# First half's feed-forward operand normalised behind its merge; second half's y, x and old operand on GpSimd's DMA queue

## The chip, the cores and the metric

The kernel runs on one core of a Trainium2 chip. The metric is the device time of one execution in microseconds (us). PE is TensorE (matrix products), DVE is VectorE, ACT is ScalarE, POOL is GpSimd, SP is SyncE, which here only issues DMAs. ACT and POOL issue DMAs too.

## The reference

One decoder layer over 1024 tokens of width 1024, in fp32: two mixers side by side, merged by gates, then a SwiGLU feed-forward block, then a norm.

```python
u = rmsnorm(h, norm1_g); proj = u @ w_in
y_a = rwkv7_mix(token_shift(p_rwkv, tshift_mu), ...)      # a recurrence over tokens
y_b = dsa_attention(q, k, v, q_idx, k_idx, w_idx)          # causal, top-256 keys
g_a, g_b = jnp.split(jax.nn.sigmoid(p_gate), 2, axis=-1)
h = h + (g_a * (y_a @ w_o_rwkv) + g_b * (y_b @ w_o_att)) @ w_out
z = rmsnorm(h, norm2_g) @ w_ffn_in                         # 1024 x 5632
z_gate, z_up = jnp.split(z, 2, axis=-1)
h = h + (jax.nn.silu(z_gate) * z_up) @ w_ffn_out           # 2816 x 1024
return rmsnorm(h, normf_g)
```

rmsnorm divides each token's row by its root mean square and multiplies it by a gain for each column.

## The kernel before

**Tiles and products.** The tokens are worked in two halves of 512. Activations lie transposed: a tile is 128 channels by 512 tokens, and eight of them are one half of a 1024-wide operand. To keep fp32 precision each product runs in three passes on a high and a low part of both operands: `split` writes `hi` on ACT (L117) and `lo = x - hi` on DVE (L118), and `mm3` issues hi x hi (L143), hi x lo (L144) and lo x hi (L148), 24 matmuls for eight blocks of 128, 18 for six. Weights stream in through `wst` (three buffers) and are split the same way into `whi` and `wlo` (two buffers each). Products go to PSUM: `acc()` takes one of three banks in turn, `mix()` one of five. `tmp()` is a ring of four tiles.

**Order.** PE's order is written by hand: the program issues the matmuls of the long chains (rwkv, attention) itself and between them pumps work from a queue named `fill`. On the other engines and the DMA queues a scheduler sets the order beforehand; each works its list in order, and waits where the next entry isn't ready.

**The stages around the change.** While rwkv and attention of the second half run, `fill` holds `merge` and `ffn` of the first half. `merge(0)` forms h, stores it as `d_h`, and writes z = h times the gain of norm2 as the parts zhi and zlo, not yet divided by the root mean square. That divisor comes as a `row` (1 x 512, spread over the partitions; L276) only when `ffn_in` is under way, so each gate product pg and up product pu of `ffn_in` is multiplied by `row` as it leaves PSUM (L1289 to L1293). The feed-forward width is worked in three groups of 8, 8 and 6 blocks (`GROUPS`), each with `ffn_in` (j over the blocks, two products each) and `ffn_out` (d over eight output blocks, added to `d_h`; L1315 loads the old value, L1321 adds, L1325 stores). Beside the last `ffn_out` of the first half the helper `scaled` multiplies z by `row`, splits it anew and stores it as `d_z` (L1442 to L1445).

Then `merge(1)` runs for the second half (it loads y at L1201 and x in `load_x`), and `joint` works the third group of both halves together with fewer products, as in Strassen's method. It needs sums and differences of both halves' operands: `old(k)` loads a block of `d_z` (L1543), L1534 normalises the second half, L1560 and L1566 form the sums. The results go to `d_f`. `reload` brings them back, and the final `ffn_out` adds the last product of the first half, in three `acc` banks of which the second half's `ffn_in`, pumped ahead and suspended, holds two.

Of the kernel before, what the change touches and what calls it, by code (L numbers as in the profile page):

```python
# [24 lines left out]
HT = 512  # L25
# [25 lines left out]
def block_kernel(ctx: ExitStack, tc: tile.TileContext, ins: dict, outT: bass.AP, outR: bass.AP, stop=None, dbg=None):  # L51
# [55 lines left out]
    def acc():  # L107
        return psA.tile([128, HT], F32, tag="acc", name="acc")
# [4 lines left out]
    def tmp():  # L113
        return tp.tile([128, HT], F32, tag="tmp", name="tmp")
# [167 lines left out]
        A.activation(hi, x, AF.Copy, scale=g)  # L282
        V.scalar_tensor_tensor(lo, x, g, hi.bitcast(F32), op0=ALU.mult, op1=ALU.subtract)

    def load_x(half, h, js):
        src = ins["xT"][:, half * HT:(half + 1) * HT].rearrange("(k p) t -> p k t", p=128)
        for j in js:
            SY.dma_start(h[:, j, :], src[:, j, :])

# [906 lines left out]
    def merge(half, zp, zs, between=None):  # L1196
        yt = yhi, ylo = act_tiles(zp, "y", ("s0", "s1"))
        mt = act_tiles(zp, "m", ("s2", "s3"))
        for j in range(8):
            t = ylo[:, j, :].bitcast(F32)  # L1200
            SY.dma_start(t, (d_ya if j < 4 else d_yb)[half][j % 4])  # L1201
            split(yhi[:, j, :], ylo[:, j, :], t)
        yield (-30, -56)[half]
        for d in range(8):
            w = weights(ins["w_o"][d])
            ga, gb = tmp(), tmp()
            SY.dma_start(ga, d_g[half][d])
# [12 lines left out]
        h = zp.tile([128, 8, HT], F32, tag="s0", name="h")  # L1220
        load_x(half, h, range(8))
        sq = Rms(h)
        zt = zhi, zlo = act_tiles(zp, "z", ("s1", "s3")) if half == 0 else (None, None)
        pss = []
        if half == 0:
            pss = [acc(), acc()]
            yield from mm3_last(pss, [weights(ins["w_out"][d]) for d in range(2)], mt, 8)
        for d in range(8):
            if d == 4 and between:
                between()  # L1230
            if d < len(pss):
# [12 lines left out]
        for d in range(8):  # L1244
            V.scalar_tensor_tensor(zlo[:, d, :], h[:, d, :], par[:, P_N2 + d:P_N2 + d + 1],
                                   zhi[:, d, :].bitcast(F32), op0=ALU.mult, op1=ALU.subtract)
        zs.extend((zt, sq))
# [12 lines left out]
                T.matmul(ps, whi[:, k, :], alo[:, k, :], start=False, stop=k == 7)  # L1260
            yield 8

    def ffn_in(f, zs, gi):

        z, sq = zs[:2]
        g0, gn = GROUPS[gi]
        for j in range(gn):
            pg, pu = acc(), acc()
            src = [ins["w_ffn_in"][2 * (g0 + j) + i] for i in range(2)]
            if gi == j == 0 and sq is not None:  # L1270
                ws = [weights(x) for x in src]
                first_ = mm3_late([pg, pu], ws, z)
                for i, n in enumerate(first_):
                    yield n
                    if i == 3:
                        sq.columns()
                zs.append(sq.row())
                yield 4
            else:
                yield from mm3(pg, weights(src[0]), z)  # L1280
                yield from mm3(pu, weights(src[1]), z)
            t = tmp()
            if sq is None:
                A.activation(t, pg, AF.Tanh, scale=0.5)
                V.scalar_tensor_tensor(t, t, 1.0, pg, op0=ALU.add, op1=ALU.mult)
                V.scalar_tensor_tensor(t, pu, 0.5, t, op0=ALU.mult, op1=ALU.mult)
            else:
                row, x = zs[2], tmp()
                V.tensor_tensor(x, pg, row, op=ALU.mult)  # L1289
                A.activation(t, x, AF.Tanh, scale=0.5)  # L1290
                V.scalar_tensor_tensor(t, t, 1.0, x, op0=ALU.add, op1=ALU.mult)
                V.scalar_tensor_tensor(x, pu, 0.5, row, op0=ALU.mult, op1=ALU.mult)
                V.tensor_tensor(t, t, x, op=ALU.mult)  # L1293
            split(f[0][:, j, :], f[1][:, j, :], t)

    def ffn_out(half, zp, f, gi, sqs=None):
        gn = GROUPS[gi][1]
        final = sqs is not None
        if final:
            h = zp.tile([128, 8, HT], F32, tag="s1", name="h")  # L1300
            sqs.append(Rms(h))
            for d in range(8):
                G.dma_start(h[:, d, :], d_h[half][d])

        def w(d):
            return weights(ins["w_fo1"][d] if final else ins["w_fo0"][gi, d], gn)

        pss = [acc() for _ in range(1 if final else 2)]
        yield from mm3_last(pss, [w(d) for d in range(len(pss))], f, gn, within=half == 1)
        for d in range(8):  # L1310
            if final:
                t = h[:, d, :]
            else:
                t = tmp()
                SY.dma_start(t, d_h[half][d])  # L1315
            if d < len(pss):
                ps = pss[d]
            else:
                ps = acc()
                yield from mm3(ps, w(d), f, nk=gn)  # L1320
            V.tensor_tensor(t, t, ps, op=ALU.add)  # L1321
# [100 lines left out]
            V.tensor_scalar(out[:, 512:768], hT[:, 512:768], rs, None, op0=ALU.mult)  # L1422
            SY.dma_start(outR[:, 512:1024], out[:, 512:1024])

    def ffn(half, zp, zs, tags, after=None):

        for gi in range(JOINT):
            f = act_tiles(zp, "f", tags)
            yield from ffn_in(f, zs, gi)
            side = iter(after() if after and gi == JOINT - 1 else ())  # L1430
            for n in ffn_out(half, zp, f, gi):
                yield n
                next(side, None)
            for _ in side:
                pass

    def scaled(z, row):

        zhi, zlo = z
        for k in range(8):  # L1440
            hi, lo, t = zhi[:, k, :], zlo[:, k, :], tmp()
            V.tensor_tensor(t, hi.bitcast(F32), lo.bitcast(F32), op=ALU.add)  # L1442
            V.tensor_tensor(t, t, row, op=ALU.mult)
            split(hi, lo, t)
            SY.dma_start(d_z[k], t)  # L1445
            yield

    class Planes:


        def __init__(self, *aps):
            self.aps = aps

        def __getitem__(self, at):
            return self.aps[at[1]][:, at[2]]

    def parts(t):
        return [t[:, k, :] for k in range(4)], [t[:, 4 + k, :] for k in range(4)]

    def joint(z0, zp0, zs1, zp1, md, after):  # L1460

# [78 lines left out]

        def old(k):
            t = tmp()
            SY.dma_start(t, d_z[k])  # L1543
            return t

        def less(k):
# [24 lines left out]
        run(*fill)  # L1571
        fill.clear()
        credit[0] = 0
        b11, b21 = ([[x[:, k, :] for k in ks] for x in z0] for ks in (range(4), range(4, 8)))
        with tc.high_priority():
            first_rows(0)
            first_rows(1)
# [2 lines left out]
            m2(j)  # L1580

        def rest():
            t3, T3 = pair(zp0, "s2")
            for k in range(4):
                split(t3[:, k, :], t3[:, 4 + k, :], less(k))
            t4, T4 = pair(zp0, "s0")
# [53 lines left out]
    def reload(half, f):  # L1640
        for j in range(GROUPS[JOINT][1]):
            t = f[1][:, j, :].bitcast(F32)
            SY.dma_start(t, d_f[half][j])
            split(f[0][:, j, :], f[1][:, j, :], t)

    def chain(*gens):
# [61 lines left out]
    def ready():  # L1708
# [5 lines left out]
        zps.append(opened("left", "zp0"))  # L1714
        m = merge(0, zps[0][1], z0)
        next(m)
        fill.append(chain(m, ffn(0, zps[0][1], z0, ("s2", "s0"), lambda: scaled(z0[0], z0[2]))))

    rwkv(1, rp, consts, ready)
    wq[0] = SY  # L1720
# [111 lines left out]
```

## Time and profile before

| what | value |
|---|---|
| time, median of three runs | 1784.09 us (1781.21 to 1787.59) |
| profiled execution | 1781.26 us, span 1779.4, granted clock 0.985 |
| PE busy | 1699.8 us |
| DVE busy | 1149.3 us |
| ACT busy | 869.2 us |
| POOL busy | 104.3 us |
| waits of PE for L1321's tmp | 25.7 us in two waits |
| waits of PE for L1321's h | 13.1 us in seven waits |

The span is the time between the first and the last instruction of the profiled execution. A timeline row gives start, length, engine, line, operation, what it writes and reads, and in brackets how long the engine stood before it and which instruction ended that. Consecutive matmuls overlap: each row's length is longer than the distance to the next.

### The profile page before, as it was taken

To read this page: it belongs to the slowest core of one execution; us is meant where nothing else is said; L and a number is where in the kernel's file an instruction comes from. 1 tells how busy PE (TensorE), PEld (TensorE's weight loads), DVE (VectorE), ACT (ScalarE), POOL (GpSimd) and SP (SyncE) were. 2 spreads that over 40 slices of the span, in tenths; PEclk is the share of its full clock that TensorE was granted. 3 is DMA by queue.
4 is the path that set the end of the run, shared out by engine and by line. 5 is a ranking of instruction groups with operands and counts; after the bars stand their busy time and mean duration, and the time that the engine had idled before them with its cause. 6 is when DMAs were issued, how large, how long until landed. Compare 5 with 4: busy or idle time off the path is not lost.

```text
span 1779.4 us, 26713 instructions
## 1 busy us (share of the span) xinstructions
PE 1699.8 (96%) x10000; PEld 1395.9 (78%) x10000; DVE 1149.3 (65%) x2242; ACT 869.2 (49%) x1685; POOL 104.3 (6%) x127
## 2 busy tenths in 40 slices
PE   8999999999999999999999999699699997999998
PEld 7888888888877777787878888577578775888888
DVE  6789899865577578778856655665775543433334
ACT  5365997543555887654343655323233342222322
POOL 0000000010021110001002110000000000000001
PEclk9999999999999999999999999899899999999999
DMA  5542344454376336633437652556622442453363
GB/s 209 183 132 80 107 112 146 141 131 151 110 223 180 111 122 199 202 111 97 123 113 230 156 148 71 184 170 196 183 86 72 148 151 68 166 166 107 113 192 110
DMA packets 148033, 253.45 MB, mean 142 GB/s; under 512 B 49680, under 2 KB 71888, under 8 KB 147776
## 3 DMA queue, kind: packets, MB, share of 16 engines
q1 hardware_dynamic: 123824, 176.53, 31.8%
q10 hardware_dynamic: 16128, 48.60, 8.5%
q0 software_dynamic: 7952, 26.61, 5.6%
q8 instruction: 79, 1.29, 0.3%
q14 instruction: 50, 0.41, 0.1%
HBM read 193.45 MB, written 58.25 MB: 141 GB/s over the span
## 4 chain that ended last, share of the span: by engine, by line
PE 78%; DVE 9%; DMA 6%; ACT 3%; issue 2%; POOL 1%; SPq 0%; ACTq 0%; DVEq 0%; POOLq 0%
PE acc L143 18%; PE acc L144 18%; PE acc L148 17%; PE acc L161 3%; DVE wlo L118 2%; PE mix L1106 2%; PE mix L947 2%; PE mix L1082 2%; PE mix L1096 2%; DMA d_h<-tmp 1%; ACT whi L117 1%; PE mix L1507 1%; PE mix L1505 1%; PE mix L1504 1%; PE mix L143 1%
## 5 line engine op out<-in xcount | busy, mean ns | idle before, releaser
L118 DVE TENSOR_TENSOR wlo<-wst,whi 128x1024 fp32r<-128x1024 f32 (+1 forms) x203 | 247.9, 1222 | 245.1 <-ACT whi L117 116.2
L117 ACT ACTIVATE whi<-wst 128x1024 fp32r<-128x1024 f32 (+1 forms) x203 | 212.4, 1048 | 288.6 <-PE acc L144 229.7
L143 PE MATMUL acc<-u1hi,whi 128*128 128x512 f32 x320 | 128.4, 401 | 0.0
L144 PE MATMUL acc<-u1lo,whi 128*128 128x512 f32 x320 | 125.5, 392 | 0.0
L143 PE MATMUL acc<-u0hi,whi 128*128 128x512 f32 (+1 forms) x320 | 122.8, 387 | 0.0
L144 PE MATMUL acc<-u0lo,whi 128*128 128x512 f32 (+1 forms) x320 | 121.3, 382 | 0.0
L143 PE MATMUL acc<-fhi,whi 128*128 128x512 f32 x234 | 94.4, 404 | 26.8 <-DVE tmp L1321 12.8
L143 PE MATMUL acc<-s,whi 128*128 128x512 f32 x256 | 100.6, 393 | 2.1 <-DVE h L1321 2.1
L144 PE MATMUL acc<-s,whi 128*128 128x512 f32 x256 | 100.6, 393 | 0.0
L143 PE MATMUL acc<-zhi,whi 128*128 128x512 f32 x240 | 97.0, 404 | 0.0
L144 PE MATMUL acc<-zlo,whi 128*128 128x512 f32 x240 | 94.3, 393 | 0.0
L144 PE MATMUL acc<-flo,whi 128*128 128x512 f32 x234 | 93.3, 399 | 0.0
L148 PE MATMUL acc<-u1hi,wlo 128*128 128x512 f32 x320 | 81.8, 395 | 0.0
L148 PE MATMUL acc<-u0hi,wlo 128*128 128x512 f32 (+1 forms) x320 | 78.6, 384 | 0.0
L143 PEld LDWEIGHTS acc<-fhi,whi 128*128 128x128 f32 x234 | 44.9, 192 | 39.8 <-issue 27.9
L997 ACT ACTIVATE junkl<-kept,z 128x1024 int8<-128x1024 int16 (+1 forms) x64 | 69.4, 1085 | 4.7 <-DVE kept L966 4.4
L143 PEld LDWEIGHTS acc<-u1hi,whi 128*128 128x128 f32 x320 | 60.3, 189 | 12.7 <-issue 0.9
L1087 ACT ACTIVATE L<-L,mx 128x128 f32<-128x128 f32 (+7 forms) x64 | 49.5, 774 | 40.9 <-DVE mx L1084 40.3
L143 PEld LDWEIGHTS acc<-u0hi,whi 128*128 128x128 f32 x320 | 60.2, 188 | 11.9 <-issue 0.4
L144 PEld LDWEIGHTS acc<-u1lo,whi 128*128 128x128 f32 x320 | 60.4, 189 | 11.3
L144 PEld LDWEIGHTS acc<-u0lo,whi 128*128 128x128 f32 x320 | 60.2, 188 | 11.0
L148 PEld LDWEIGHTS acc<-u1hi,wlo 128*128 128x128 f32 x320 | 58.9, 188 | 12.5 <-issue 0.9
(429 smaller groups left out, 3974.7 us busy)
## 6 DMA issues: line engine op xcount, KB each, us to landing
wst<-in_w_ffn_in SPq DMA_DIRECT2D x61, 512.0 KB, 4.1
wst<-in_w_in ACTq DMA_DIRECT2D x36, 512.0 KB, 5.2
wst<-in_w_in SPq DMA_DIRECT2D x27, 512.0 KB, 3.9
wst<-in_w_fo SPq DMA_DIRECT2D x25, 512.0 KB, 4.0
k<-d_k POOLq DMA_DIRECT2D x24, 512.0 KB, 8.4
h<-in_xT SPq DMA_DIRECT2D x32, 256.0 KB, 5.2
d_g<-tmp ACTq DMA_DIRECT2D x32, 256.0 KB, 3.0
tmp<-d_g SPq DMA_DIRECT2D x32, 256.0 KB, 4.0
```

Of the source, the lines that this page charges most:

```text
L117: A.activation(hi, x, AF.Copy)
L118: V.tensor_tensor(lo, x, hi.bitcast(F32), op=ALU.subtract)
L143: T.matmul(ps, whi[:, wk + k, :], ahi[:, ak + k, tok], start=k == 0, stop=False)
L144: T.matmul(ps, whi[:, wk + k, :], alo[:, ak + k, tok], start=False, stop=False)
L148: T.matmul(ps, wlo[:, wk + k, :], ahi[:, ak + k, tok], start=False, stop=k == nk - 1)
L161: T.matmul(ps, w[:, k, :], a[:, k, tok], start=k == 0 and j == 0, stop=k == nk - 1 and j == 2)
L947: T.matmul(ps[:, :w], iq[:, h, :], ik[:, i, c:c + w], start=i == 0, stop=i == 1)
L997: A.activation(junka[:, :n], y, AF.Sign, bias=z[:, i:i + 1], accum_out=cnt[:, i:i + 1])
L1082: T.matmul(ps[:, :w], q[bi // 2][:, e, bi % 2 * 128:bi % 2 * 128 + 128], k[:, i, e, c:c + w], start=i == 0, stop=i == 1)
L1087: A.activation(L[:, :n], L[:, :n], AF.Exp, scale=-1.0, bias=last, accum_out=sm[:, bi, e:e + 1])
L1096: T.transpose(ps[:, j * 128:(j + 1) * 128], L[:, (c + j) * 128:(c + j + 1) * 128], ident)
L1106: T.matmul(py[64 * e:64 * e + 64, bi * 128:(bi + 1) * 128], v[:, j, 64 * e:64 * e + 64], pts[e][j // 4][:, j % 4, :], start=j == b, stop=j ...
```

## The change

The first half's operand is normalised once, right behind the first gate and up products of `ffn_in`: `normalise` multiplies h by gain and row into tiles, stores them as `d_z` and splits them into `za` and `zb` (in the slots s2 and s0, the latter h's own). j = 0 and 1 still use zhi and zlo and are multiplied by `row` as they leave PSUM; from j = 2 on the products use the normalised operand, and leave PSUM by the shorter way of the second half (L1327 to L1329 of the new kernel). `scaled` is gone. The tiles f take the slots s1 and s3, which zhi and zlo leave, and are allocated when j = 1 is done; the splits of j = 0 are held until then. The loads of y and x of the second half, of `d_z` in `old`, and `reload` are issued by POOL (`G`) instead of SP (`SY`). The final `ffn_out` of the first half uses `mix` banks instead of `acc`.

```diff
-            SY.dma_start(t, (d_ya if j < 4 else d_yb)[half][j % 4])
+            (G if half else SY).dma_start(t, (d_ya if j < 4 else d_yb)[half][j % 4])
...
-        load_x(half, h, range(8))
+        load_x(half, h, range(8), G if half else SY)
...
+    def normalise(zp, sq, row):
+
+        h = sq.h
+
+        def one(k, out):
+            V.scalar_tensor_tensor(out, h[:, k, :], par[:, P_N2 + k:P_N2 + k + 1], row, op0=ALU.mult, op1=ALU.mult)
+            SY.dma_start(d_z[k], out)
+
+        low, ts = zp.tile([128, 8, HT], F32R, tag="s2", name="za"), []
+        for k in range(4):
+            one(k, h[:, k, :])
+            split(low[:, k, :], low[:, 4 + k, :], h[:, k, :])
+        for k in range(4):
+            ts.append(tmp())
+            one(4 + k, ts[k])
+        high = zp.tile([128, 8, HT], F32R, tag="s0", name="zb")
+        for k in range(4):
+            split(high[:, k, :], high[:, 4 + k, :], ts[k])
+        return [Planes(*(a + b)) for a, b in zip(parts(low), parts(high))]
+
+    def ffn_in(zp, tags, zs, gi, box):
+
         g0, gn = GROUPS[gi]
+        sq, held = zs[1], []
+        early = 2 if gi == 0 and sq is not None else 0
         for j in range(gn):
             pg, pu = acc(), acc()
             src = [ins["w_ffn_in"][2 * (g0 + j) + i] for i in range(2)]
...
+            if j < early:
+                if j == 0:
+                    ws = [weights(x) for x in src]
+                    for i, n in enumerate(mm3_late([pg, pu], ws, zs[0])):
+                        yield n
+                        if i == 3:
+                            sq.columns()
+                    row = sq.row()
+                    z = normalise(zp, sq, row)
+                    yield 4
+                else:
+                    yield from mm3(pg, weights(src[0]), zs[0])
+                    yield from mm3(pu, weights(src[1]), zs[0])
+                    zs[0] = z
+                x, t = tmp(), tmp()
                 V.tensor_tensor(x, pg, row, op=ALU.mult)
...
+            else:
+                yield from mm3(pg, weights(src[0]), zs[0])
+                yield from mm3(pu, weights(src[1]), zs[0])
+                t = tmp()
+                A.activation(t, pg, AF.Tanh, scale=0.5)
+                V.scalar_tensor_tensor(t, t, 1.0, pg, op0=ALU.add, op1=ALU.mult)
+                V.scalar_tensor_tensor(t, pu, 0.5, t, op0=ALU.mult, op1=ALU.mult)
+            held.append((j, t))
+            if j >= early - 1:
+                if not box:
+                    box.append(act_tiles(zp, "f", tags))
+                for i, t in held:
+                    split(box[0][0][:, i, :], box[0][1][:, i, :], t)
+                held = []
...
-            h = zp.tile([128, 8, HT], F32, tag="s1", name="h")
+            h = zp.tile([128, 8, HT], F32, tag="s2", name="h")
...
-        pss = [acc() for _ in range(1 if final else 2)]
+        bank = mix if final else acc
+        pss = [bank() for _ in range(1 if final else 2)]
...
-            side = iter(after() if after and gi == JOINT - 1 else ())
-            for n in ffn_out(half, zp, f, gi):
-                yield n
-                next(side, None)
...
-    def scaled(z, row):
...
         def old(k):
             t = tmp()
-            SY.dma_start(t, d_z[k])
+            G.dma_start(t, d_z[k])
...
     def reload(half, f):
...
-            SY.dma_start(t, d_f[half][j])
+            G.dma_start(t, d_f[half][j])
```

PE's matmuls stand in the same order in both kernels. What moves is the order on the other engines.

**DVE at the first products of ffn_in.** Names: nq and x_... are tiles of rwkv, row the divisor, za and zb the normalised operand. Before, from the weight splits of j = 0 on:

```order
L118 TENSOR_TENSOR wlo<-wst,whi 128x1024 x2
L1289 TENSOR_TENSOR tmp<-acc,row 128x512
L1291 SCALAR_TENSOR_TENSOR tmp<-tmp 128x512
L613 TENSOR_SCALAR x_8289<-x_8248,hb 128x256
L1292 SCALAR_TENSOR_TENSOR tmp<-acc,row 128x512
```

And now:

```order
L118 TENSOR_TENSOR wlo<-wst,whi 128x1024 x2
L1280 SCALAR_TENSOR_TENSOR h<-h,par,row 128x512 x3
L118 TENSOR_TENSOR za<-h,za 128x512 x3
L1280 SCALAR_TENSOR_TENSOR h<-h,par,row 128x512
L1280 SCALAR_TENSOR_TENSOR tmp<-h,par,row 128x512 x2
L621 TENSOR_SCALAR nq<-mix 128x256
L118 TENSOR_TENSOR wlo<-wst,whi 128x1024
L118 TENSOR_TENSOR za<-h,za 128x512
L1280 SCALAR_TENSOR_TENSOR tmp<-h,par,row 128x512 x2
L586 TENSOR_SCALAR x_8281<-x_8281 128x1024
L613 TENSOR_SCALAR x_8323<-x_8282,hb 128x256
L118 TENSOR_TENSOR zb<-tmp,zb 128x512 x4
```

The eviction of j = 0's gate product (L1289, now L1318) follows only behind these.

**DVE a little later, at rwkv's nr** (a tile that L630 copies from PSUM, POOL works on, and ACT and DVE split). Before:

```order
L623 TENSOR_TENSOR x_8289<-x_8289,x_8183 128x1024
L630 COPY nr<-mix 128x16
L596 COPY PC<-P 128x2x4
L598 COPY PC<-P 128x2x2 x2
L666 TENSOR_TENSOR AR<-x_8185,P 128x8x64 x2
L118 TENSOR_TENSOR wlo<-wst,whi 128x1024
L118 TENSOR_TENSOR nr_8356<-nr,nr_8356 128x2x8
```

And now:

```order
L623 TENSOR_TENSOR x_8323<-x_8323,x_8181 128x1024
L630 COPY nr<-mix 128x16
L1320 SCALAR_TENSOR_TENSOR tmp<-tmp 128x512
L666 TENSOR_TENSOR AR<-x_8183,P 128x8x64
L118 TENSOR_TENSOR nr_8390<-nr,nr_8390 128x2x8
L666 TENSOR_TENSOR AR<-x_8183,P 128x8x64
L118 TENSOR_TENSOR wlo<-wst,whi 128x1024
```

The weight split wlo (that of j = 2's gate product) stood ahead of nr's subtraction and stands behind it now.

**DVE at the last ffn_out of the first half and the start of merge(1).** Before:

```order
L118 TENSOR_TENSOR wlo<-wst,whi 128x1024 x2
L118 TENSOR_TENSOR ylo<-ylo,yhi 128x512 x4
L1442 TENSOR_TENSOR tmp<-zhi,zlo 128x512 x2
L1443 TENSOR_TENSOR tmp<-tmp,row 128x512 x2
L1442 TENSOR_TENSOR tmp<-zhi,zlo 128x512
L118 TENSOR_TENSOR zlo<-tmp,zhi 128x512 x2
L1443 TENSOR_TENSOR tmp<-tmp,row 128x512
L1442 TENSOR_TENSOR tmp<-zhi,zlo 128x512 x2
L118 TENSOR_TENSOR zlo<-tmp,zhi 128x512
L1443 TENSOR_TENSOR tmp<-tmp,row 128x512 x2
L118 TENSOR_TENSOR zlo<-tmp,zhi 128x512
L1321 TENSOR_TENSOR tmp<-tmp,acc 128x512
```

And now:

```order
L118 TENSOR_TENSOR ylo<-ylo,yhi 128x512 x6
L1364 TENSOR_TENSOR tmp<-tmp,acc 128x512
L118 TENSOR_TENSOR wlo<-wst,whi 128x1024 x2
L118 TENSOR_TENSOR ylo<-ylo,yhi 128x512 x2
L1364 TENSOR_TENSOR tmp<-tmp,acc 128x512
```

The eviction (L1321, now L1364) no longer stands behind the work of `scaled`.

**SP at the same place.** Before:

```order
L1445 DMA d_z<-tmp 128x512
L1143 DMA d_yb_117<-tmp 128x512
L1201 DMA ylo<-d_ya_115 128x512 x4
L1201 DMA ylo<-d_yb_117 128x512 x4
L1445 DMA d_z<-tmp 128x512 x2
L124 DMA wst<-in_w_o 128x1024 x2
L1445 DMA d_z<-tmp 128x512 x3
L1315 DMA tmp<-d_h_109 128x512
```

And now:

```order
L1131 DMA d_s<-tmp 8x128
L1137 DMA tmp<-d_s 64x512 x2
L1358 DMA tmp<-d_h_109 128x512 x2
L124 DMA wst<-in_w_o 128x1024
L1143 DMA d_yb_117<-tmp 128x512
L1358 DMA tmp<-d_h_109 128x512
```

The loads of `d_h` for the eviction (L1315, now L1358) stand right behind attention's last reload (L1137); y's loads are on POOL's list.

More of the change, by code (lines that the diff above doesn't have):

```diff
@@ L283, in gsplit, with load_x @@
         V.scalar_tensor_tensor(lo, x, g, hi.bitcast(F32), op0=ALU.mult, op1=ALU.subtract)
-    def load_x(half, h, js):
+    def load_x(half, h, js, eng=SY):
         src = ins["xT"][:, half * HT:(half + 1) * HT].rearrange("(k p) t -> p k t", p=128)
         for j in js:
-            SY.dma_start(h[:, j, :], src[:, j, :])
+            eng.dma_start(h[:, j, :], src[:, j, :])
     rows = [None, None]
@@ L1261, in mm3_late, with __init__, __getitem__, parts @@
             yield 8
-    def ffn_in(f, zs, gi):
-        z, sq = zs[:2]
+    class Planes:
+        def __init__(self, *aps):
+            self.aps = aps
+        def __getitem__(self, at):
+            return self.aps[at[1]][:, at[2]]
+    def parts(t):
+        return [t[:, k, :] for k in range(4)], [t[:, 4 + k, :] for k in range(4)]
+    def normalise(zp, sq, row):
[15 more added lines that the diff above has]
+    def ffn_in(zp, tags, zs, gi, box):
         g0, gn = GROUPS[gi]
+        sq, held = zs[1], []
+        early = 2 if gi == 0 and sq is not None else 0
         for j in range(gn):
@@ L1269, in ffn_in @@
             src = [ins["w_ffn_in"][2 * (g0 + j) + i] for i in range(2)]
[L1270 to L1273, printed above, removed]
-                    yield n
[L1275 to L1288, printed above, removed]
+            if j < early:
[13 more added lines that the diff above has]
+                x, t = tmp(), tmp()
                 V.tensor_tensor(x, pg, row, op=ALU.mult)
@@ L1318, in ffn_out @@
             else:
-                ps = acc()
+                ps = bank()
                 yield from mm3(ps, w(d), f, nk=gn)
@@ L1423, in finish_out, with ffn @@
             SY.dma_start(outR[:, 512:1024], out[:, 512:1024])
-    def ffn(half, zp, zs, tags, after=None):
+    def ffn(half, zp, zs, tags):
         for gi in range(JOINT):
-            f = act_tiles(zp, "f", tags)
-            yield from ffn_in(f, zs, gi)
-            side = iter(after() if after and gi == JOINT - 1 else ())
-            for n in ffn_out(half, zp, f, gi):
-                yield n
-                next(side, None)
-            for _ in side:
-                pass
-    def scaled(z, row):
[L1439 to L1458, printed above, removed]
+            f = []
+            yield from ffn_in(zp, tags, zs, gi, f)
+            yield from ffn_out(half, zp, f[0], gi)
     def joint(z0, zp0, zs1, zp1, md, after):
@@ L1573, in joint @@
         credit[0] = 0
-        b11, b21 = ([[x[:, k, :] for k in ks] for x in z0] for ks in (range(4), range(4, 8)))
+        b11, b21 = ([[x.aps[k] for k in ks] for x in z0] for ks in (range(4), range(4, 8)))
         with tc.high_priority():
@@ L1582, in rest @@
         def rest():
-            t3, T3 = pair(zp0, "s2")
+            t3, T3 = pair(zp0, "s1")
             for k in range(4):
                 split(t3[:, k, :], t3[:, 4 + k, :], less(k))
-            t4, T4 = pair(zp0, "s0")
+            t4, T4 = pair(zp0, "s3")
             for k in range(4):
@@ L1716, in ready @@
         next(m)
-        fill.append(chain(m, ffn(0, zps[0][1], z0, ("s2", "s0"), lambda: scaled(z0[0], z0[2]))))
+        fill.append(chain(m, ffn(0, zps[0][1], z0, ("s1", "s3"))))
     rwkv(1, rp, consts, ready)
@@ L1734, in block_kernel @@
     smd.close()
-    fj = act_tiles(zp0, "f", ("s2", "s0"))
+    fj = act_tiles(zp0, "f", ("s1", "s0"))
     reload(0, fj)
```

1 line of the change is left out of this document (removed).

## The prediction

> **What bounds the kernel now.** I read the page's engine line first, then PE's waits, then windows over the stages that the diff touches, then the timelines there. TensorE is busy 96% of the span, and its instructions stand in the same order before and after; only names and banks differ. So the change can move time only through PE's idle time, some 80 us.
>
> ```profile
> span 1779.4 us, 26713 instructions
> ...
> PE 1699.8 (96%) x10000; PEld 1395.9 (78%) x10000; DVE 1149.3 (65%) x2242; ACT 869.2 (49%) x1685; POOL 104.3 (6%) x127
> ```
>
> PE's waits by releaser (total, times, longest): the two big kinds end at L1321, the add that evicts a product of ffn_out from PSUM. Two waits of 12.9 and 12.8, and seven of about 1.9.
>
> ```profile
> PE acc L143 <- DVE tmp L1321: 25.7, 2, 12.9
> PE acc L143 <- DVE h L1321: 13.1, 7, 2.1
> ```
>
> Windows (PE busy is the first number after the length): the stretch where the change adds work, 800 to 900, is nearly full; the one where it removes `scaled` is not.
>
> ```profile
> 800.00:900.00 100.00, 97.79 (x564) 79.71 (x562) 82.11 (x168) 37.50 (x60) 7.57 (x2) 0.98 0.40 116
> 1100.00:1200.00 100.00, 82.89 (x435) 64.67 (x434) 62.49 (x95) 37.00 (x58) 0.00 (x0) 0.91 0.50 164
> ```
>
> **A: normalise behind the merge (803 to 840 us).** Timeline rows of PE, DVE and POOL around the first two j of ffn_in (start, length, engine, line):
>
> ```profile
> 811.58 0.50 PE L143 MATMUL acc<-zhi,whi 128*128 128x512 f32 x1
> 821.04 1.98 PE L148 MATMUL acc<-zhi,wlo 128*128 128x512 f32 x8
> 827.54 0.73 PE L647 MATMUL mix<-nrT,ind 16*128 16x256 f32 x4 [1.58 <-ACT nrT L641]
> ...
> 805.95 0.69 DVE L1289 TENSOR_TENSOR tmp<-acc,row 128x512 f32<-128x512 f32 x1 [1.04 <-ACT row L276]
> 809.81 0.69 DVE L586 TENSOR_SCALAR x<-x 128x1024 f32<-128x1024 f32 x1
> 811.92 0.41 DVE L621 TENSOR_SCALAR nq<-mix 128x256 f32<-128x256 f32 x1
> 812.25 1.21 DVE L118 TENSOR_TENSOR wlo<-wst,whi 128x1024 fp32r<-128x1024 f32 x1
> 817.19 0.16 DVE L630 COPY nr<-mix 128x16 f32<-128x16 f32 x1
> 830.41 1.27 DVE L649 TENSOR_TENSOR x<-x,mix 128x512 f32<-128x512 f32 x2
> ...
> 817.49 5.17 POOL L634 TENSOR_TENSOR nr<-nr,mhalf 128x16 f32<-128x16 f32 x1 [18.34 <-DVE nr L630]
> ...
> 1263.80 1.41 DVE L1534 SCALAR_TENSOR_TENSOR h<-h,par,row 128x512 f32<-128x512 f32 x2
> ```
>
> Before, L1289 at 805.95 frees the bank of j=0's gate product, well ahead of 811.58, where PE starts j=1's up product in that same bank (three acc banks, four products). After, DVE has the whole normalise ahead of this eviction (now L1318). Its multiply is the operation of L1534, of which two take 1.41, so some 0.68 each; two 128x512 operations on two tiles take 1.27 (L649), and since each start overlaps the end before by about 0.1, their pitch is 0.60. Eight multiplies 5.4, eight subtractions 4.8, and between them nq (L621) 0.3, wlo 1.1, L586 0.6 and one L613, a 256-wide operation like nq's, 0.3: 12.5 us. L1318 starts at 805.95 + 12.5 = 818.5 and ends at 819.2; PE stands 7.6 us.
>
> It doesn't end there. From L1318's end to L630 DVE has nine operations of 256 or 512 columns at 0.3 to 0.6 (four scans, the rest of two evictions, three L613), the small copies, the next L1318 and a 1024-wide product of 1.1, together some 7.2 us: L630 at 826.4 instead of 817.19. POOL's 5.17 us and ACT's split bring nr to 831.8, and in the new order the wlo of j=2's gate product stands behind nr's subtraction, where before it stood ahead of it. That wlo is ready at about 833.9; PE wanted it at 821.04. So the delay grows to 12.9. The wait for nrT (1.58) goes, ACT's next whi, behind the late splits of f, takes about 1: **+12**. The low end is the bank alone, 7.6; the high end 15, if each restart also pays slow matmuls. Behind 840 PE has no slack to give it back (windows).
>
> The normalise's ACT splits (eight, 0.6 each) run beside DVE's; its eight stores replace those of `scaled` on SP, which has nothing urgent there. From j=2 on, 14 evictions lose two DVE operations each, about 17 us of DVE; PE waits for none of them in its list of waits, so nothing.
>
> **B: `scaled` removed (1123 to 1160).**
>
> ```profile
> 1152.48 0.77 PE L143 MATMUL acc<-yhi,whi 128*128 128x512 f32 x1 [12.86 <-DVE tmp L1321]
> 1153.05 0.63 PE L144 MATMUL acc<-ylo,whi 128*128 128x512 f32 x1
> 1160.11 0.50 PE L143 MATMUL acc<-yhi,whi 128*128 128x512 f32 x1 [0.30 <-ACT whi L117]
> ...
> L1096 PE MATMUL mix<-kc,L x31: 270/272/275, 1099.8 to 1113.6; 128*128 128x128 f32 x31
> ...
> 1143.04 1.28 DVE L1442 TENSOR_TENSOR tmp<-zhi,zlo 128x512 f32<-128x512 f32 x2
> 1151.65 0.68 DVE L1321 TENSOR_TENSOR tmp<-tmp,acc 128x512 f32<-128x512 f32 x1
> ...
> 1123.26 1.09 SPq L1137 DMA_DIRECT2D tmp<-d_s  x2
> 1144.96 3.33 SPq L1445 DMA_DIRECT2D d_z<-tmp  x3
> 1148.39 0.37 SPq L1315 DMA_DIRECT2D tmp<-d_h  x1
> ```
>
> PE waits from 1139.6 for a bank. L1321 comes at 1151.65, behind `scaled` on DVE (from 1143.04) and behind its stores on SP, which hold the load of d_h until 1148.39. After, SP issues this load right behind attention's last reload (L1137, 1123 to 1125), and DVE has only six splits of y, L1321's successor and two wlo: eviction at about 1136, wlo at 1139, two more splits of y and the second eviction at 1140.8. I place the product that started at 1160.11 at about 1144: **-16**. It needs y by about 1136. GpSimd may issue the y loads when attention's tiles are free (its L1096 matmuls end at 1113.6), since nothing else is queued on it; only the last waits for its own store, and a load of 2.7 to 7.1 (rows in C) puts it at 1135 to 1139.5. Hence -12 to -17.
>
> **C and D: old operand on GpSimd's queue (1256 to 1322).**
>
> ```profile
> 1285.38 0.76 PE L143 MATMUL acc<-fhi,whi 128*128 128x512 f32 x1 [12.83 <-DVE tmp L1321]
> 1284.56 1.87 DVE L1321 TENSOR_TENSOR tmp<-tmp,acc 128x512 f32<-128x512 f32 x3
> tmp<-d_z SPq DMA_DIRECT2D x12, 256.0 KB, 2.8
> ...
> 1386.97 4.38 POOL L1303 DMA_DIRECT2D h<-d_h  x8 [129.63 <-PE mix L1507]
> DMA to landing us min/median/max: 2.7/4.9/7.1
> L1060 POOL DMA_DIRECT2D v<-d_v x12: 752/761/791, 507.6 to 1059.7; - x12
> DMA to landing us min/median/max: 3.3/5.8/12.8
> ```
>
> (The first landing row is that of the h loads, the second that of v.) The second big wait stays: DVE works without a break from 1262 to L1321 at 1284.56, and that order is unchanged. The eight loads feed this chain with 0.2 to 2 us of slack; a load takes 4.9 on POOL against 2.8 on SP, but issues earlier, no longer behind weights. I take +1 (-1 to +5) and +0.5 (0 to +3) for the last four in the joint stage. The x loads are wanted one by one, each behind a product of 24 matmuls (5.4 us), so even 7.1 for the first costs under 2; reload's come ahead of 136 pumped matmuls, 31 us. Both at nothing.
>
> By the Trainium skill (SBUF — State Buffer, "SBUF: two separate sides") a transfer issued from GpSimd stands still while DVE is in a two-port mode, since its descriptors can't be written; its figures are about 620 ns alone and 3100 beside such a copy. By that C would be worse by up to eight times 2.5, an estimate of 20 us. The trace shows steady issues of 752 to 791 ns beside a busy DVE, which speaks against it.
>
> **E: final ffn_out in mix banks (1457 to 1504).**
>
> ```profile
> 1458.76 0.47 PE L143 MATMUL acc<-fhi,whi 128*128 128x512 f32 x1 [0.87 <-ACT whi L117]
> 1464.92 0.47 PE L143 MATMUL acc<-fhi,whi 128*128 128x512 f32 x1 [1.80 <-DVE h L1321]
> 1497.42 0.63 PE L143 MATMUL acc<-fhi,whi 128*128 128x512 f32 x1
> 1503.90 0.64 PE L143 MATMUL acc<-s,whi 128*128 128x512 f32 x1 [2.06 <-DVE h L1321]
> ...
> 1463.22 0.96 DVE L118 TENSOR_TENSOR wlo<-wst,whi 128x768 fp32r<-128x768 f32 x1 [3.46 <-PE acc L148]
> 1464.09 0.68 DVE L1321 TENSOR_TENSOR h<-h,acc 128x512 f32<-128x512 f32 x1
> ...
> wst<-in_w_fo SPq DMA_DIRECT2D x16, 384.0 KB, 4.7
> ```
>
> The suspended ffn_in of the second half holds two acc banks, so each product waits until L1321 has emptied the last: seven waits, 13.1 us. Five mix banks end that. A matmul takes 0.227 at speed (eight in 1.98 in the L148 row of A, whose last runs 0.39). Seven products of 18 take 28.6 us; they and the waits now take 1503.90 - 1458.8 = 45.1, the surplus being waits, drain and some 20 matmuls at 0.43 behind 1497. Gain 13.1 to 16.5; weights (three slots, splits of under 1 us on each engine) should follow. **-15**.
>
> The slow matmuls behind 1152.48 and 1497.42 are a halved clock: 0.43 apart instead of 0.23. The Trainium skill (TensorE: Matmul & The Clock Gate, Part 1) says that PE falls to half rate after an idle window of about 3.4 us and needs as long to come back. By it A's stall costs 1.7 more, an estimate; 1497 shows it behind waits of only 2, so gaps needn't be long.
>
> **Sum**: +12 - 16 + 1 + 0.5 - 15 = -17.5. The profiled execution took 1781.3 (span 1779.4 and 1.9 around it), so 1763.8; the median of the runs is 2.8 above it, 1784.1, so 1766.6.
>
> **Rivals.**
> - *A stops at the bank stall or is swallowed by later slack*: +7.6 or less gives 1762 or lower. For it: DVE gets lighter from j=2. Against: PE's 97.8% at 800 to 900.
> - *B's stall only changes its owner*: y is late, or whi (1.9 us there before). Without B: 1783, no change. It needs y 16 us late; against it, its tiles are free 20 us before.
> - *E is paced by weights*: the loads take 4.7 us against 4.1 a product; if they went one at a time, 0.6 x 7 is lost: 1771.
> - *Slower: GpSimd's queue takes one load at a time*, 4.9 each. Eight loads of y then take 39 us from 1114, to 1153: B gives nothing. Eight of d_z in C end at 1296 instead of 1282, +14; four in D +4. With A and E: +12 + 0 + 14 + 4 - 15 = +15, 1799. It decides from some 3.5 us a load. Against it: eight loads issued within 4.38 us all landed within 7.1 of issue, under 1.5 us each. (The rule of the SBUF page of the Trainium skill, above, would work this way, at one place or at all.)
>
> **How the numbers follow.** My forecast 0.57 (own range 1758 to 1774), A small 0.13, E paced by weights 0.12, B void 0.09, GpSimd one at a time 0.09. 0.3% is 5.3 us, about what a measurement can tell: faster means below 1778.8. Forecast, small A and paced E are faster, 0.82; B void is the same, 0.09; the last is slower, 0.09. The range 1754 to 1781 leaves out GpSimd's case, most of B void's upper side and a thin tail below.
>
> **What would show it.** A: a PE wait of 6 to 9 us at about 811 for L1318, then one for wlo at about 830. B: no wait above 3 at 1136 to 1160 (all times 12 later). C: the wait of 12.8 still there, ending at L1364. E: no waits for L1364's h. If y's splits wait for DMA, or C's wait passes 18, GpSimd's queue is at work and I am wrong; so too if A's delay passes 20, where rwkv's chain took it further.

## The result and the profile after

The changed kernel takes 1752.71 us (median of 4 runs, 1751.27 to 1757.02) against 1782.80 for the kernel before (4 runs, 1781.21 to 1787.59): a ratio of 0.9831, 95% interval 0.9804 to 0.9858. It is 30 us faster; 17.5 were forecast, and the time lies 1.3 us below the range. The profiled execution took 1751.42 us.

The page's first lines, of the changed kernel:

```profile
span 1749.6 us, 26678 instructions
...
PE 1691.1 (97%) x10000; PEld 1391.5 (80%) x10000; DVE 1129.0 (65%) x2206; ACT 867.5 (50%) x1685; POOL 124.4 (7%) x167
```

PE's waits by releaser (total, times, longest). L1364 and L1318 are the new numbers of the additions and evictions:

```profile
PE acc L143 <- DVE tmp L1364: 13.5, 2, 13.2
PE acc L143 <- DVE tmp L1318: 7.6, 1, 7.6
```

One of the two waits of 12.9 is gone, so are the seven for h, and one of 7.6 is new. The timelines of A (PE, DVE, POOL):

```profile
818.24 0.79 PE L143 MATMUL acc<-zhi,whi 128*128 128x512 f32 x1 [7.56 <-DVE tmp L1318]
818.83 0.63 PE L144 MATMUL acc<-zlo,whi 128*128 128x512 f32 x1
829.01 1.07 PE L148 MATMUL acc<-za,wlo 128*128 128x512 f32 x4
835.69 0.73 PE L647 MATMUL mix<-nrT,ind 16*128 16x256 f32 x4 [1.74 <-ACT nrT L641]
...
817.51 0.67 DVE L1318 TENSOR_TENSOR tmp<-acc,row 128x512 f32<-128x512 f32 x1
830.26 1.22 DVE L118 TENSOR_TENSOR wlo<-wst,whi 128x1024 fp32r<-128x1024 f32 x1
...
825.47 3.82 POOL L634 TENSOR_TENSOR nr<-nr,mhalf 128x16 f32<-128x16 f32 x1 [27.27 <-DVE nr L630]
```

And of B, C and E (PE):

```profile
1146.28 0.50 PE L143 MATMUL acc<-yhi,whi 128*128 128x512 f32 x1 [0.21 <-DVE tmp L1364]
1149.55 0.50 PE L143 MATMUL acc<-yhi,whi 128*128 128x512 f32 x1 [0.23 <-ACT whi L117]
...
1275.26 0.76 PE L143 MATMUL acc<-fhi,whi 128*128 128x512 f32 x1 [13.25 <-DVE tmp L1364]
...
1448.00 1.52 PE L148 MATMUL mix<-fhi,wlo 128*128 128x512 f32 x6
1452.08 1.52 PE L148 MATMUL mix<-fhi,wlo 128*128 128x512 f32 x6
```

In E the products now follow each other every 4.08 us, 18 matmuls at 0.227, where they took 6.16 with the wait.

PE's matmuls stand in one order in all these kernels, so the trace can be cut at the same matmuls. The cuts: rwkv's L604 next to A; its L647; the first L161 row of the first half's second `ffn_out`; merge(1)'s reduction L256; the first L161 row of the final `ffn_out`; that of the second half's first `ffn_out`; the end of the last matmul; the end of the span. Lengths in us, from the profiled execution of each kernel:

```
                 ahead     A  to ffn_out     B     C+D      E    rest  close
before           811.0  16.5      297.6  129.9   198.6  108.3   210.6   6.9
after            810.0  25.6      294.8  114.0   196.7   88.9   210.2   9.3
acc_again        811.3  25.6      294.9  114.0   196.3  106.5   210.2   9.3
mix_only         811.1  16.5      297.1  131.1   199.2   88.9   211.1   6.9
scaled_stores    810.8  16.5      297.1  117.8   199.6  106.5   210.9   6.9
all_on_sp        808.7  25.6      295.0  115.8   195.4   88.9   210.2   6.9
old_on_sp        811.6  25.6      294.8  115.6   196.7   88.9   210.2   8.4
h_late           815.8  25.2      294.7  114.4   199.9   88.9   210.2   9.3
long_evict       816.2  25.2      297.2  114.1   197.7   88.9   210.2   9.4
evict_first      825.0  14.9      297.4  114.6   196.6   88.9   210.2   9.3
fill_first       812.1  25.6      294.9  115.3   189.7   88.9   210.2   9.3
both_sp          819.8  14.9      297.4  117.8   184.7   88.9   211.5   6.9
fill_sp          814.1  25.3      294.7  116.5   185.0   88.9   210.4   6.9
fill_y           820.4  25.3      294.7  114.6   184.5   88.9   210.2   7.5
```

In the first column every engine works the same list in all but evict_first and both_sp (where the early eviction puts waits ahead of the first cut), and it still runs from 808.7 to 820.4: that is the scatter of the times, and it has nothing to do with the change. The other columns repeat to within about 1.7 us where the code is the same (B with y on GpSimd's queue 114.0 to 115.6, E with acc banks 106.5 to 108.3), most of them much closer. After against before: -1.0, +9.1, -2.8, -15.9, -1.9, -19.3, -0.4, +2.4, together -29.8.

### The profile page after: what moved, and what is told of

The parts are those of the page before. It is cut to its first block, busy times and chain, and to the rows that moved or that the text cites. A ratio compares the mean times of both kernels' runs of the same rounds, so it can differ in the third digit from the quotient of the medians.

```text
span 1749.6 us, 26678 instructions
## 1 busy us (share of the span) xinstructions
PE 1691.1 (97%) x10000; PEld 1391.5 (80%) x10000; DVE 1129.0 (65%) x2206; ACT 867.5 (50%) x1685; POOL 124.4 (7%) x167
## 4 chain that ended last, share of the span: by engine, by line
PE 84%; DVE 5%; issue 4%; DMA 3%; ACT 3%; POOL 1%; ACTq 0%; POOLq 0%; DVEq 0%; SPq 0%
PE acc L143 19%; PE acc L144 19%; PE acc L148 18%; PE acc L161 3%; PE mix L1106 2%; PE mix L1082 2%; PE mix L1096 2%; PE mix L947 2%; PE mix L143 2%; PE mix L144 2%; PE mix L148 2%; ACT whi L117 1%; DVE wlo L118 1%; PE mix L1522 1%; PE mix L1520 1%
## 5 line engine op out<-in xcount | busy, mean ns | idle before, releaser
L143 PE MATMUL acc<-fhi,whi 128*128 128x512 f32 x192 | 76.6, 399 | 13.8 <-DVE tmp L1364 13.2
L144 PE MATMUL acc<-flo,whi 128*128 128x512 f32 x192 | 75.6, 394 | 0.0
L148 PEld LDWEIGHTS acc<-u0hi,wlo 128*128 128x128 f32 x320 | 58.1, 188 | 11.9 <-issue 0.7
L148 PE MATMUL acc<-s,wlo 128*128 128x512 f32 x256 | 63.6, 390 | 0.0
L144 PEld LDWEIGHTS acc<-s,whi 128*128 128x128 f32 x256 | 48.1, 188 | 10.0
```

The lines of the kernel that those rows point to most:

```text
L143: T.matmul(ps, whi[:, wk + k, :], ahi[:, ak + k, tok], start=k == 0, stop=False)
L144: T.matmul(ps, whi[:, wk + k, :], alo[:, ak + k, tok], start=False, stop=False)
L148: T.matmul(ps, wlo[:, wk + k, :], ahi[:, ak + k, tok], start=False, stop=k == nk - 1)
```

## The experiments

**E undone (acc_again).**

```diff
-        bank = mix if final else acc
+        bank = acc
```

> The changed kernel with the final ffn_out of the first half in acc banks again, as before the change. Theory 1 (the prediction's term E: seven waits for the last free bank and some drain, 15 us): 15 us slower than the changed kernel, about 1768. Theory 2 (reading of the two traces: 19.3 us between the start of that stage and the same matmul of the next one, the slow matmuls behind the waits included): 19 us slower, about 1772. Rival (the stage got shorter because GpSimd issues reload's loads and DVE has less to do): no difference, 1753 to 1756. PE's waits for L1364's h come back seven times at about 1.9 under theories 1 and 2.

Measured 1775.37 us (6 runs), ratio to the kernel before 0.9953 (0.9932 to 0.9974). The profiled execution is the fastest of the six (1769.88). In it E grows from 88.9 to 106.5, 17.6 us, and every other stretch stays. PE's waits:

```profile
PE acc L143 <- DVE h L1364: 13.1, 7, 2.1
```

By the trace this lies between the two theories: 13.1 of waits for the bank; the rest is the wait of 0.9 at the start, drain (the end of a last matmul that no next one overlaps) and slow matmuls. The medians are 22.7 apart, further than either theory, with 5 us of scatter in them. The rival (reload's queue, lighter DVE) falls.

**E alone (mix_only).** The kernel before with the same choice of banks.

```diff
-        pss = [acc() for _ in range(1 if final else 2)]
+        bank = mix if final else acc
+        pss = [bank() for _ in range(1 if final else 2)]
...
-                ps = acc()
+                ps = bank()
```

> The kernel before with one edit: the final ffn_out of the first half takes mix banks. Theory 1: 15 us off, 1768. Theory 2: 19 us off, 1764, all of it between the stage's first matmul at about 1454 and the next stage, nothing ahead of it. Rival (the banks alone don't help while reload's loads stand on SP and weights pace the products): under 5 us off, 1778 or more.

Measured 1762.89 us, ratio 0.9883 (0.9856 to 0.9911). E is 88.9 again, 19.3 less than before: theory 2. The 1.7 between 19.3 and 17.6 is slow matmuls: the kernel before has them on both sides of 1503.90, acc_again only ahead of its last wait, and scaled_stores (below), which keeps the acc banks and also has 106.5, only behind it. Two rows of the kernel before, the eighth matmul behind 1503.90 and the tenth:

```profile
1506.89 0.63 PE L144 MATMUL acc<-s,whi 128*128 128x512 f32 x1
1507.62 0.40 PE L144 MATMUL acc<-s,whi 128*128 128x512 f32 x1
```

So some two thirds of the whole gain come from a choice of banks that has nothing to do with normalising.

**B without DVE's part (scaled_stores).**

```diff
-            hi, lo, t = zhi[:, k, :], zlo[:, k, :], tmp()
-            V.tensor_tensor(t, hi.bitcast(F32), lo.bitcast(F32), op=ALU.add)
-            V.tensor_tensor(t, t, row, op=ALU.mult)
-            split(hi, lo, t)
-            SY.dma_start(d_z[k], t)
+            SY.dma_start(d_z[k], zhi[:, k, :].bitcast(F32))
```

> The kernel before with scaled cut to its stores: d_z is written from zhi without addition, multiplication or split (this leaves the division by the root mean square out of what joint and the later products use). The stores stand on SP, y's and x's loads on SP as before. Theory 1 (B: DVE's work of scaled and the stores that wait for it hold the eviction): the wait of 12.9 at 1152 falls under 3, 13 to 16 us off, about 1767 to 1770. Rival (y's loads on SP behind the last store of attention set the stage, so GpSimd's queue is what brings B): the wait shrinks by half at most, 5 to 8 us off, 1775 to 1778.

Measured 1770.48 us (7 runs), ratio 0.9931 (0.9908 to 0.9953). B falls to 117.8, by 12.0. PE's timeline there:

```profile
1136.97 0.50 PE L143 MATMUL acc<-fhi,whi 128*128 128x512 f32 x1 [1.54 <-ACT whi L117]
1141.98 0.50 PE L143 MATMUL acc<-yhi,whi 128*128 128x512 f32 x1 [1.03 <-DVE tmp L1321]
1147.22 0.47 PE L143 MATMUL acc<-yhi,whi 128*128 128x512 f32 x1 [2.23 <-DVE tmp L1211]
```

The wait of 12.9 is 1.0: it was DVE's work of `scaled` and the stores that wait for it (the run doesn't tell these two apart). The 2.2 for L1211 behind it waits in its turn for a load of d_g (DVE stood 4.46 for it), which SP issues at 1139.94, behind y's loads and two of weights.

**All loads back on SP (all_on_sp).**

```diff
-            (G if half else SY).dma_start(t, (d_ya if j < 4 else d_yb)[half][j % 4])
+            SY.dma_start(t, (d_ya if j < 4 else d_yb)[half][j % 4])
...
-            G.dma_start(t, d_z[k])
+            SY.dma_start(t, d_z[k])
```

(and x and reload likewise)

> The changed kernel with y, x, old operand and reload on SP's queue again. Theory 1 (prediction: the queues cost 1.5 us in C and D and help B by no more than 4): between 2 us faster and 4 slower, 1751 to 1757. Theory 2 (the traces: two waits of 2.5 and 1.7 late in joint went away, which the old operand's loads on SP may have caused): 2 to 4 us slower, 1755 to 1757, with waits of PE at L1519 back late in joint. Rival (B hangs on GpSimd's queue): 5 to 16 us slower, with a wait of PE at the first products of merge(1) for y.

Measured 1751.85 us, ratio 0.9827 (0.9797 to 0.9857): no difference from the changed kernel that the times can tell. The stretches tell more: the close is 2.4 shorter. B is 1.9 longer without GpSimd's queue: 115.8 here, up to 117.8 in the later runs with y on SP, against 114.0 to 115.6 with y on GpSimd. C+D is 1.3 shorter, no more than it scatters. Neither the rival on B nor theory 2 on D holds: the wait for u (ACT's copy of a product, L1630) late in joint didn't come back. The other of its two waits never went: the changed kernel has it too (1.71, below), all_on_sp at 1.1.

**One queue back (old_on_sp).**

```diff
-            G.dma_start(t, d_z[k])
+            SY.dma_start(t, d_z[k])
```

> The changed kernel with only the old operand's twelve loads back on SP: GpSimd issues 119 transfers, between the 91 of the kernel before and the 131 of the changed one. If GpSimd's closing drain grows with the number of its transfers: 5.8 us (3.53 + 28 of 40 parts of 3.27), the span's end 1.4 us or so behind that of a kernel with 91. If it is a step: 3.5 or 6.8. For C: the stretch from 1245 to the final ffn_out within 1 us of the changed kernel's 196.7 if the prediction's +1 for the queue was too much, 1.5 shorter if it was right.

One execution, span 1751.8 us. C+D is 196.7 as in the changed kernel: +1 for the queue was too much there. (PE's wait at C is 12.8 instead of 13.2, so the queue costs 0.4 at that place.) GpSimd's closing drain by its line (min, median and max in ns), first of the kernel before, with 91 transfers on that engine:

```profile
L1827 POOLq DRAIN  x3: 45/93/3532, 1774.2 to 1779.1; - x3
```

then of the changed kernel, with 131:

```profile
L1842 POOLq DRAIN  x3: 45/93/6800, 1742.0 to 1749.3; - x3
```

of this kernel, with 119:

```profile
L1842 POOLq DRAIN  x3: 45/102/5820, 1745.2 to 1751.5; - x3
```

and of fill_y (below), with 99:

```profile
L1842 POOLq DRAIN  x3: 45/102/4188, 1740.3 to 1745.8; - x3
```

The longest drain is 3.53, 6.80, 5.82 and 4.19 us: a straight line, 82 ns a transfer. The step is excluded.

**h's loads later (h_late).**

```diff
-            h = zp.tile([128, 8, HT], F32, tag="s2", name="h")
+            h = zp.tile([128, 8, HT], F32, tag="s0", name="h")
...
-    fj = act_tiles(zp0, "f", ("s1", "s0"))
+    fj = act_tiles(zp0, "f", ("s1", "s2"))
```

> The changed kernel with the final ffn_out's tile h in slot s0 (zb's) instead of s2 (za's), f in s1 and s2; h's eight loads of d_h then wait for the last use of zb, about 20 us later. Theory (the 2.1 us that went late in joint came from these loads: before, they were issued at 1387 to 1391, just ahead of a weight load at 1391.6 that ACT waited 4.6 for; in the changed kernel at 1366 to 1370): PE's waits of about 2.5 for u and 1.7 for the sum of m5 at the last j of joint come back, the stretch from 1275 to ffn_out's first matmul is 2 to 3 us longer. Rival (they went for another reason, as shorter queues on SP): no change there.

One execution, span 1758.4 us, of which 5.8 stand ahead of the edit. C+D grows by 3.2. Of the two waits, that for u is back in full; the other, which the changed kernel has too, is shorter. PE's rows of this kernel, then the one of the changed kernel:

```profile
1395.51 0.50 PE L1519 MATMUL mix<-s,sw 128*128 128x512 f32 x1 [2.54 <-ACT u L1630]
1400.90 0.50 PE L1519 MATMUL mix<-s,sw 128*128 128x512 f32 x1 [0.78 <-DVE tmp L1641]
...
1392.11 0.50 PE L1519 MATMUL mix<-s,sw 128*128 128x512 f32 x1 [1.71 <-DVE tmp L1641]
```

GpSimd's row for h and ACT's for the last weights, from the timelines of this kernel:

```profile
1382.39 4.31 POOL L1345 DMA_DIRECT2D h<-d_h  x8 [9.26 <-PE mix L1522]
1393.92 1.06 ACT L117 ACTIVATE whi<-wst 128x1024 fp32r<-128x1024 f32 x1 [4.77 <-DMA wst<-in_w_ffn_in]
```

and the same two rows of the changed kernel:

```profile
1365.84 4.31 POOL L1345 DMA_DIRECT2D h<-d_h  x8 [53.63 <-PE mix L1522]
1385.75 1.06 ACT L117 ACTIVATE whi<-wst 128x1024 fp32r<-128x1024 f32 x1 [2.08 <-DMA wst<-in_w_ffn_in]
```

So what D won came from a tag: in slot s2 the final tile h is free some 11 us sooner (counted from merge(1)'s L256 in each run), and its 2 MB no longer run into the last weights. The edit also lets three of the reloads of f go ahead of h's loads; no run tells the two apart.

**The longer eviction kept (long_evict).**

```diff
                 t = tmp()
+                if sq is not None:
+                    x = tmp()
+                    V.tensor_tensor(x, pg, zs[2], op=ALU.mult)
+                    A.activation(t, x, AF.Tanh, scale=0.5)
...
```

> The changed kernel with the longer eviction kept for all 16 j of the first half (row is applied twice to 14 of them): some 17 us of DVE work back, spread from 840 to 1120. The prediction costed this relief at nothing. If that holds, the stretch from rwkv's L647 to the last ffn_out of the first half stays within 0.7 us of the changed kernel's 294.8. If the lighter DVE gave back part of A's delay, it grows by 1 to 3 us toward the 297.7 of the kernel before.

One execution, span 1758.9 us. From L647 to the last ffn_out: 297.2 against 294.8, so the lighter DVE gives back 2.3. PE's wait for rwkv's MT in this stretch, 0.4 in the changed kernel, shows most of it:

```profile
PE mix L702 <- DVE MT L706: 1.9, 1, 1.9
```

**A's stall taken away (evict_first).**

```diff
                     row = sq.row()
+                    x, y = mix(), mix()
+                    V.tensor_tensor(x, pg, row, op=ALU.mult)
+                    V.scalar_tensor_tensor(y, pu, 0.5, row, op0=ALU.mult, op1=ALU.mult)
                     z = normalise(zp, sq, row)
```

> The changed kernel with one edit in ffn_in: j = 0's two products are multiplied by row into two mix banks ahead of normalise, so both acc banks come free at once. Theory 1 (A: the stall of 7.6 us is the bank, and 1.6 us of half-rate matmuls follow from it): no wait at the up product of j = 1, 5 to 9 us off the changed kernel, 1744 to 1748. Rival (DVE is late for rwkv anyway: nr and the weight splits come behind normalise whatever the bank does): PE waits for DVE or ACT within 15 us of there instead, under 2 us off, 1751 or more.

Measured 1756.96 us, ratio 0.9823 (0.9796 to 0.9850), the same as the changed kernel's. PE's waits in this stretch:

```profile
PE mix L574 <- ACT x L582: 4.2, 1, 4.2
PE mix L604 <- DVE x L680: 1.3, 1, 1.3
```

and the first of them in PE's timeline:

```profile
816.78 2.07 PE L574 MATMUL mix<-wa,wup 64*128 64x256 f32 x6 [4.15 <-ACT x L582]
```

The wait of 7.6 is gone, and one of 4.2 stands earlier, one of 1.3 later. From rwkv's L802, ahead of all this (801.6 here, 794.6 in the changed kernel), to the second `ffn_out` it takes 335.7 against 335.9. PE waits 3.2 less there, but its busy time is 3.0 longer (329.0 against 326.0), as matmuls run slow behind the new waits: the one that follows the 4.2 at 819.37, for example.

```profile
819.37 0.63 PE L144 MATMUL acc<-zlo,whi 128*128 128x512 f32 x1
```

The rival has the time right, but not the reason. The wait for nrT (1.74 in the changed kernel) is gone, so nr wasn't late here. The 4.2 comes from the edit: its two mix banks are missing to rwkv, and on ACT the splits of za, which wait for normalise, now stand ahead of the reads (L582) that free the others:

```profile
813.89 1.96 ACT L117 ACTIVATE za<-h 128x512 fp32r<-128x512 f32 x3 [2.01 <-DVE h L1280]
815.75 1.85 ACT L582 ACTIVATE x<-mix,hb 128x256 f32<-128x256 f32 x6
```

What A would cost with a free bank and nothing else moved, no run shows.

**C's order (fill_first).**

```diff
         pump(4)
+        run(*fill)
+        fill.clear()
+        credit[0] = 0
         t1, T1 = pair(zp1, "s2")
...
             split(b22[:, k, :], b22[:, 4 + k, :], h[:, 4 + k, :])
-        run(*fill)
-        fill.clear()
-        credit[0] = 0
```

> The changed kernel with one edit in joint: the rest of fill (the last products of ffn_out and their additions) is issued ahead of the loops that form joint's sums, not behind them; PE's order stays. Theory 1 (C: the wait of 13.2 is DVE's queue order alone): that wait falls under 3 us, 10 to 13 us off, 1740 to 1743. Rival (joint's first products need the sums, so the wait only moves behind the last product of ffn_out): a wait of 8 or more at L1519, under 4 us off, 1749 or more.

Measured 1747.86 us, ratio 0.9779 (0.9748 to 0.9809). The wait of 13.2 is gone, C+D 7.0 shorter. This lies between theory and rival: the sums come later now, and PE waits for DVE in joint. PE's and DVE's timelines:

```profile
1314.37 0.77 PE L1519 MATMUL mix<-s,sw 128*128 128x512 f32 x1 [5.26 <-DVE tmp L1641]
...
1295.18 0.69 DVE L1584 TENSOR_TENSOR tmp<-tmp 128x512 f32<-128x512 f32 x1 [0.46 <-DMA tmp<-d_z]
```

**Both, without GpSimd's queue (both_sp).** The edits of evict_first, fill_first and all_on_sp together.

> Both edits (evict_first, fill_first) with y, x, old operand and reload on SP's queue, as the traces point to: GpSimd's closing drain takes 6.80 us in the profiles with 131 of its transfers and 3.53 in those with 91, and the span ends 2.4 us later behind the last store. If the gains add: 7 + 12 + 2.4 off the changed kernel, 1731 (1726 to 1737). If A's or C's stall moves instead of going: 1740 or more.

Measured 1744.38 us, ratio 0.9756 (0.9728 to 0.9783): the gains don't add up to 1731, the stalls moved. C+D is 184.7, another 5.0 less than fill_first. Once joint's sums stand on the path, the old operand is faster from SP: DVE waits 7.5 us for it in fill_first, 4.2 here. (y, x and reload moved too; no run tells what they add.) DVE's longest waits for it, in fill_first and here:

```profile
DVE tmp L1578 <- DMA tmp<-d_z: 6.4, 2, 5.4
...
DVE tmp L1585 <- DMA tmp<-d_z: 4.2, 2, 2.5
```

**The order without early eviction (fill_sp), and with y on GpSimd (fill_y).** fill_first with all four kinds of loads on SP; the second leaves `(G if half else SY)` for y.

> The order edit of fill_first, with y, x, old operand and reload on SP's queue, and no early eviction: 5 us less behind C than fill_first if it was GpSimd's queue that held the sums there (both_sp: 184.7 against 189.7 from merge's last reduction to the final ffn_out), and 2.4 less at the end; early eviction was worth 0.3 us by the traces, so about the time of both_sp, ratio to the kernel before 0.975. If early eviction mattered after all, 3 us or more slower than that, 0.977 or more.

> As fill_sp, but y alone stays on GpSimd's queue (99 transfers). The traces give y's place there 1.8 us at the start of merge(1) (113.97 against 115.79 to its last reduction); the closing drain may take up to 0.7 of it. 1 us faster than fill_sp, within what the times can tell; a ratio within 0.001 of it.

Measured 1745.63 us, ratio 0.9783 (0.9754 to 0.9811), and 1742.56 us, ratio 0.9751 (0.9722 to 0.9780). fill_sp's ratio is on the side where early eviction would have mattered, but its interval holds both_sp's 0.9756, and by the traces it takes 335.5 from L802 to the second `ffn_out` against 335.2: the 0.3 expected. The two ratios lie 0.003 apart where 0.001 was expected. fill_y's C+D is 184.5, B 114.6, 1.9 less than fill_sp's, the close 7.5. It has the lowest of the nine ratios and beats both given kernels; its lead over both_sp and fill_sp lies within the intervals.

## Why the prediction was wrong, point by point

**Direction and places held.** The five places were the right ones. B is 15.9 of 16 forecast, by the mechanism named. C's wait stayed (13.25). A's first stall came to the tenth, 7.56 against 7.6, and not by luck: DVE's list from the first multiply (804.99) to L1318 (817.51) took the 12.5 that were added up. What failed is one wait that never came (A) and sizes, nearly all in one direction, so the sum fell 12 us short.

**E, mis-sized: 15 was taken, 19.3 measured (17.6 in acc_again).** The step gave "13.1 to 16.5" and took 15 between. The measured end of the stage wasn't its end: I counted from 1458.8 to 1503.90, so the wait of 0.87 at the start and the eight slow matmuls behind 1503.90 (0.63 long, some 0.2 too much each, 1.6) were left out. 16.5 + 0.9 + 1.6 is 19.0.

**A, one term wrong: +12 forecast, +9.1 measured.** The step that failed is "the wlo of j=2's gate product stands behind nr's subtraction", which the section on the change says too. That row of the order is the split of j = 2's *up* product: it runs at 830.26, while PE's hi x lo matmuls of the gate product start at 829.01 without a wait. I had counted the splits one too few back. So the 5.3 us that this wlo was to add to the 7.6 are nothing, and the wait for nrT, which was to go, stayed (1.74). The rest of +9.1 is the stall, 7.6, slow matmuls behind it (818.24 to 820.97, 0.43 apart), 1.3, and 0.2 more for nrT. From the Trainium skill (TensorE: Matmul & The Clock Gate, Part 1) the prediction had estimated 1.7 for such a restart; the trace's 1.3 is of that size.

**"Behind 840 PE has no slack to give it back": wrong by 2.8.** The lighter DVE, costed at nothing because no wait on those evictions is listed, is worth 2.3 in the changed kernel (long_evict): DVE is one queue, and rwkv's MT (L706) comes sooner. Between the two given kernels most of the 2.8 shows up in the clock: PE's waits behind L647 are 0.7 shorter, its busy time is 2.1 shorter (296.4 to 294.3). After almost the same wait for nrT, PE ran at 0.83 before and at full rate after. A window of ten us of the kernel before (the granted clock is the third number from the end):

```profile
826.00:836.00 10.00, 8.46 (x35) 7.19 (x36) 10.00 (x16) 4.96 (x8) 0.00 (x0) 0.83 0.15 53
```

and one of the changed kernel:

```profile
834.15:844.15 10.00, 8.46 (x43) 7.14 (x44) 9.95 (x17) 4.80 (x8) 0.00 (x0) 1.00 0.23 69
```

The same page of the Trainium skill says that the window in which the gate counts runs free; by that, whether a short gap costs the half rate is chance, and part of the scatter of the first column may be of this kind. No run here tests that alone. (Of the 10.4 us by which fill_y lies behind the changed kernel in that column, 5.9 are longer busy time of PE and the rest is waits.)

**"The change can move time only through PE's idle time" was too narrow.** Of the 29.8 us, 8.7 are PE's busy time (1699.8 to 1691.1) with the same matmuls, 5.4 of them in E: fewer waits leave fewer slow matmuls, and fewer ends that no next matmul overlaps.

**C and D: +1.5 forecast, -1.9 measured.** The old operand's queue costs nothing in sum here (old_on_sp: 196.7). The gain is the wait for u, 2.5, by the slot of h, which I had read in the diff and not costed.

**The close: 0 forecast, +2.4 measured.** No step looked past the last matmul.

**The rivals.** A small A came nearest: +9.1 and the 2.8 given back are +6.3 up to the second `ffn_out`, under that rival's 7.6, and partly for the reason it gives (a lighter DVE); with it the forecast would have been 1762 or lower. "GpSimd's queue takes one load at a time" is refuted: the old operand's loads on it landed in 2.8 to 4.5 (minimum, median, maximum):

```profile
DMA to landing us min/median/max: 2.8/2.9/4.5
```

From SP's queue the median was 2.6 to 2.9 (the kernel before, old_on_sp, all_on_sp), here 2.9. Five of these loads stand beside a DVE that is busy 23.0 of 23.3 us (1252 to 1275). So the box of the Trainium skill (SBUF — State Buffer, "SBUF: two separate sides") on descriptors that wait for DVE doesn't bite with this mix of DVE operations; by its figures a load would be some 2.5 us later, an estimate. E wasn't paced by weights, and B wasn't void.

**The range** was too narrow below. The low ends of the terms add up to 26.9 us, 1757 from the median of 1784.1; the range went 3 us below that for all that had been left out. Of that, the slot, the relief and E's slow matmuls shorten the time by some 7 us together; the close and A's slow restart lengthen it by 3.7.

## What to carry to other kernels

A product that waits for its PSUM bank costs the wait, the drain and, after some of the waits, a slow restart; measure such a stage from the last matmul ahead of it to the first full-speed one behind. Taking a stall away on a busy in-order engine moved it here, wholly in A and partly in C: ask what that engine owes next, and to whom, and what the cure itself takes (two banks in A). And cost every tag in a diff: a slot decides when a transfer may start, and so what it runs into.

## What the runs showed of the hardware

GpSimd closes the program with a drain that grows by 82 ns with each transfer it has issued: 3.53 us at 91, 6.80 at 131. The last store was issued 6.2 us ahead of the span's end with 131 and 3.8 with 91, so forty loads of 256 KB moved to that queue cost 2.4 us at the end. It doesn't matter where they stand: fill_y's eight extra loads, some 600 us ahead of the end, lengthen the drain by the same 82 ns each.
